# A decoder layer in split float32 on one core: another planned product length in the front, and other engines for splits and biases around the first layer norm

## The chip, the cores and the metric

One Trainium2 chip, one of its cores. The metric is the device time of one execution in microseconds (us), the median over several executions. Engines: PE (TensorE matmul), PEld (its weight loads), DVE (VectorE), ACT (ScalarE), POOL (GpSimd), SP (SyncE, which here only issues DMAs). [...]

## What is computed

One layer over 512 tokens of width 1024 in float32. With `h = x @ w_in` (1024 x 2560) split into q, k, v, u, z (512 wide each):

```python
attn = moba_attention(rope(q), rope(k), v)         # 8 heads of 64, blocks of 256 keys
u, z = gelu(u), gelu(z)
sg   = u * (tril(w_s) @ layer_norm(z) + b_s)       # per chunk of 128 positions, 8 groups
mix  = concat(rms_norm(attn), rms_norm(sg)) @ w_out
x    = layer_norm(2**0.25 * x + mix)               # first layer norm
x    = layer_norm(2**0.25 * x + (silu(x @ w_gate) * (x @ w_up)) @ w_down)
```

The hidden width of the last line is 2816.

## The kernel before, in words

**Split products.** Every large product runs on float32 values that are split into a high part (`hi`, stored as float32r) and a low part (`lo = value - hi`). One call of `mm3` (L250) issues three matmuls into one accumulating bank: hi*hi, hi*lo, lo*hi (L252, L253, L254). A product below is one such call, on a 128x512 output. A weight chunk of 128x1024 comes by one DMA of 512 KB (class `W`, L258 on) and is split by `split` (L235): the high part on ACT (L239) or, with `near`, on DVE (L237); the low part on DVE or, with `far`, on POOL (both L240). Which group of weights takes which engine stands in `WHI` (high part on DVE) and `WPOOL` (low part on POOL). Groups are named `q0` to `q3`, `z`, `u`, and `o0` to `o7` for the eight chunks of `w_out`.

**The planner.** The program first records every operation of every engine in a class `Order`, with a cost, a due rank (`base`, mostly from the table `RANK`; a smaller one goes first among the operations that are ready) and what it reads and writes. `plan` (L108) is a list scheduler: it plays the operations through on the recorded costs, engine by engine, and the order that it finds is the order in which each engine's instructions are issued. On the chip each engine runs its list strictly in that order and waits for semaphores. Buffers of one tag are handed out in program order (`admit`), so an operation can be kept waiting by an earlier part that holds the buffers of a tag. A product is recorded at cost `MM` = 0.681, a product of the gate and up weights (three matmuls of 256 columns, L850) at `MM256` = 0.36. Transfers are recorded at max(0.46, KB/352) plus 1.9.

**The front.** `SEQ` gives the parts: `q1 a1 q0 z q2 a0 u q3 s a2 a3`. `v_step` makes 32 products for v; `q0` to `q3` (`qk_proj`, L375 on) 16 products each and then a rope, whose halves are turned by four small DMAs (L366, L367 on DVE, L369 on SP, L371 on POOL); `z` and `u` (`tok_proj`) 32 products each; `a0` to `a3` the attention of two heads each (scores L432 and L433, transposes L471, values L488); `s` the spatial gating (L566) and its norm: a square on ACT (L584), a power on POOL (L282), a scaling on DVE (L586), transposes on PE (L591). Projections have rank 15 and so fill PE between the attention's steps at rank 4. The temporaries of ropes, squares and of the gating's norm share the tag `rt` with 5 buffers.

**Output projection and first layer norm.** `out_half(4)` multiplies the gating's half by `o4` to `o7`, `out_half(0)` the attention's half by `o0` to `o3`, four token tiles t of 128 each, 8 products to a tile and half. When tile t of the second half is done, `pa_done` (L752 on) calls `layer_norm` (L685 on): add (L756), statistics (L693), scale and shift on ACT (L706), gain on DVE (L708), bias (L717). `LN1` has a letter for each tile: with `P` the bias runs on POOL, with `A` on DVE. After the bias come transposes (L766), copies (L770), splits of the operands (L239, L240), and, for t = 2 and 3, sums of blocks (`combine`, L734 on).

**Gate and up products.** The weights of the first four pairs come early (`EARLY` = 4): eight blocks, numbered 0 to 7, filled by `whole` (L833). With letter `M` of `EARLY_LO` a block goes through `split_dram` (L244): ACT writes the high part (L246) and the negative of it as the low part (L247), and a DMA from POOL (L248) fetches the same 512 KB once more and adds it to the low part. With letter `D` the low part is one subtraction on DVE (L240), as elsewhere. Blocks 0 to 3 stand in buffers of their own, 4 to 7 in the ring `wh`, `wl`. After them 11 pairs run through 7 products of 8 steps each, and then the 22 chunks of the down projection (`down_mm`), which call `mm3` with the same `MM`.

Of the kernel before, what the change touches and what calls it, by code (L numbers as in the profile page):

```python
# [29 lines left out]

SAME, CROSS, DMA_LAT, MM, MM256 = 0.15, 0.19, 1.9, 0.681, 0.36
GROW, GROW_LAT = 0.9, 10
SEQ = ('q1', 'a1', 'q0', 'z', 'q2', 'a0', 'u', 'q3', 's', 'a2', 'a3')
RANK = {"w": 5.0, "rope": 10.0, "att": 4.0, "gelu": -8.0, "z": -2.0, "s": -13.5, "fill": 15.0, "sq": -6.0, "ln": -10.5, "ffn": 8.0, "evac": 3.0}


UNITS = (2, 0, 3, 1)
NORM = "AADA"  # L40
LN1, LN2, LNT = "APAA", "ADAD", 0.3
WHI = ('o0', 'o2', 'q1')
WPOOL = ('e0', 'e1', 'e3', 'o1', 'o2', 'o4', 'z')
ROPE, ZSUB, ZMUL, ZG, ZB = "P", "P", "P", "P", "P"


class Buf:
# [139 lines left out]
def build(tc, cp, wp, ap, ps, xt, xtok, w_vqk, w_zu, w_out, w_gu, w_dn, wsp, cst, rows, cols, out):  # L187
# [14 lines left out]
    def dma(kb, fn, r, w, **k):  # L202
        od.op("SP", max(0.46, kb / 352.0), fn, r, w, **k)

    def pe(n, fn, r, w, **k):
        od.op("PE", n, fn, r, w, **k)
# [10 lines left out]
    def prob(dtype=F32):  # L217
        return work([P, S], "pr", 4, dtype)
# [4 lines left out]
    def bank(tag, bufs):  # L223
        return od.buf(ps, [P, S], F32, tag, bufs)

    def pj():
        return bank("pj", 4)
# [7 lines left out]
    def split(n, src, hi, lo, rs, ws_hi, ws_lo, far=False, lock=True, near=False, **k):  # L235
        if near:
            dve(n, lambda: V.tensor_scalar(hi(), src(), 1.0, None, op0=ALU.mult), rs, ws_hi, per=0.52, lock=True, **k)  # L237
        else:
            act(n, lambda: A.activation(hi(), src(), AF.Copy), rs, ws_hi, **k)  # L239
        either("P" if far else "D", n, lambda E: E.tensor_tensor(out=lo(), in0=src(), in1=hi().bitcast(F32),  # L240
                                                                 op=ALU.subtract), [*rs, *ws_hi], ws_lo,
               lock=lock, **k)
# [7 lines left out]
    def mm3(cost, o, lh, ll, rh, rl, start, stop, r, w, **k):  # L250
        def fn():
            PE.matmul(o(), lhsT=lh(), rhs=rh(), start=start, stop=False)  # L252
            PE.matmul(o(), lhsT=lh(), rhs=rl(), start=False, stop=False)  # L253
            PE.matmul(o(), lhsT=ll(), rhs=rh(), start=False, stop=stop)  # L254

        pe(cost, fn, r, w, **k)

    class W:  # L258


        def __init__(self, src, tag=None, mid=None, group=None):
# [10 lines left out]
            every = slice(0, WCH)  # L272
            dma(512, lambda: nc.sync.dma_start(raw.t, src), [], [raw], base=RANK["w"])
            if mid is not None:
                mid(raw)
            split(WCH, lambda: raw.t, lambda: self.hi(every), lambda: self.lo(every), [raw], hk, lk, group in WPOOL,
                  near=group in WHI, base=RANK["w"])

# [14 lines left out]
    def row(i):  # L293
        b = work([P, D], "kl", 2)
        dma(512, lambda: nc.sync.dma_start(b.t, bass.AP(tensor=rows.tensor, offset=rows.offset + 3 * S + i * D,
                                                        ap=[[0, P], [1, D]])), [], [b], base=RANK["rope"])
        return b
# [16 lines left out]
    def v_step(c, kk, raw, wh, wl):  # L314
        k = 2 * c + kk
        cs = slice(kk * 512, kk * 512 + 512)
        xr = prob()
        dma(256, lambda: nc.sync.dma_start(raw.t[:, cs], w_vqk[c][:, cs]), [], [(raw, kk)], base=RANK["w"])
        split(512, lambda: raw.t[:, cs], lambda: wh.t[:, cs], lambda: wl.t[:, cs],
              [(raw, kk)], [(wh, kk)], [(wl, kk)], base=RANK["w"])  # L320
        pieces = ((0, 1), (1, NT)) if k == 0 else ((0, NT),)
        for t0, t1 in pieces:
            def piece(t0=t0, t1=t1, ts=slice(t0 * P, t1 * P)):
                sub = [(k, t) for t in range(t0, t1)]
                dma(64 * (t1 - t0), lambda: nc.sync.dma_start(xr.t[:, ts], xt[k][:, ts]), [], [(xr, t0)], base=RANK["w"])
                split((t1 - t0) * P, lambda: xr.t[:, ts], lambda: xh.t[:, k, ts], lambda: xl.t[:, k, ts], [(xr, t0)],
# [299 lines left out]
    def out_half(c0, spare, left, done, wide=None):  # L626
        ws = [W(w_out[c0 + k], spare if k == 3 else None, group=f"o{c0 + k}") for k in range(4)]
        for t in range(NT):
            ts = slice(t * P, t * P + P)
            b = [bank("sc", 2), bank("sc", 2)] if t == wide else [pj(), pj()]  # L630
            for k in range(4):
                for hf in range(2):
                    def one(k=k, hf=hf, t=t, ts=ts, b=b, hs=slice(hf * 512, hf * 512 + 512)):
                        lh, ll, keys = left(k, t, ts)
                        mm3(MM, lambda: b[hf].t, lh, ll, lambda: ws[k].hi(hs), lambda: ws[k].lo(hs), k == 0, k == 3,
                            [*keys, *ws[k].key], [b[hf]])

                    one()
            done(t, b)
# [277 lines left out]
            self.gated(c, self.h1, self.i1, 0, -1.0)  # L917

    pairs = [Pair(p) for p in range(NP)]
    EARLY, EARLY_LO = 4, "MMMMMMMM"  # L920
    EARLY_SLOTS = (("wr", "wr"), (0, 1), ("wr", "wr"), (0, 1))
    for p in range(EARLY):
        blks = [whole(Raw(p, 3 * i, EARLY_SLOTS[p][i]), 2 * p + i) for i in range(2)]
# [47 lines left out]
    yb = [[pj(), pj()], [pj(), pj()], [bank("sc", 2), bank("sc", 2)], [bank("tp", 1), bank("pv", 1)]]  # L971
# [3 lines left out]
    def down_w(f, tag=None):  # L975
        w = W(w_dn[f], tag)
        if f < FT - 4:
            hh, hl = prob(F32R), tmp(F32R)
            parts, keys = (lambda: hh.t, lambda: hl.t), ([hh], [hl])
        else:  # L980
            i = 2 * (FT - 1 - f)
            parts, keys = (lambda: last.t[:, i, :], lambda: last.t[:, i + 1, :]), ([(last, i)], [(last, i + 1)])
        h, hi = hT[f]
        hk, neg = [(h, (hi, t)) for t in range(2)], -1.0 if f % 2 else 1.0
        act(512, lambda: A.activation(parts[0](), h.t[:, hi, :], AF.Copy, scale=neg), hk, keys[0])
        dve(560, lambda: V.scalar_tensor_tensor(out=parts[1](), in0=h.t[:, hi, :], scalar=neg, in1=parts[0]().bitcast(F32),
                                                op0=ALU.mult, op1=ALU.subtract), [*hk, *keys[0]], keys[1], lock=True)
        return w, parts, keys[0] + keys[1]

    def down_mm(f, t, hf, w):  # L990
        w, (hh, hl), keys = w
        ts = slice(t * P, t * P + P)
        hs = slice(hf * 512, hf * 512 + 512)
        mm3(MM, lambda: yb[t][hf].t, lambda: hh()[:, ts], lambda: hl()[:, ts],
            lambda: w.hi(hs), lambda: w.lo(hs), f == 0, f == FT - 1, [*w.key, *keys], [yb[t][hf]])

    TAIL = 6
    for f in range(FT - TAIL):
        w = down_w(f)
        for t in (3, 0, 1, 2):  # L1000
            for hf in range(2):
                down_mm(f, t, hf, w)
# [3 lines left out]
    def finish(t):  # L1006
        for i in range(2):
            for f in wt:
                down_mm(f, t, i, wt[f])

        def add(i, key):
            dve(512, lambda: V.scalar_tensor_tensor(out=xk.t[:, t, HV[i]], in0=xk.t[:, t, HV[i]], scalar=ALPHA,
                                                    in1=yb[t][i].t, op0=ALU.mult, op1=ALU.add),
                [yb[t][i], key], [key])

        def done(i, key):
            dma(256, lambda: nc.sync.dma_start(out[t * P:t * P + P, HV[i]], xk.t[:, t, HV[i]]), key, [])

        od.base = RANK["ffn"] - 0.1 * (t + 1)
        layer_norm(t, add, done, LN2[t])  # L1020
        od.base = RANK["ffn"]
# [68 lines left out]
```

## Time and profile before

| | |
|---|---|
| median of 3 executions | 566.88 us (566.67 to 567.62) |
| profiled execution, its own time | 566.79 us |
| its span, first to last instruction | 565.0 us, so 1.79 us lie around it |
| mean granted PE clock | 0.986 |
| PE, DVE, ACT, POOL busy | 97%, 72%, 51%, 28% of the span |
| DMA | 72.85 MB, mean 129 GB/s |

The profiled execution is 0.09 us under the median. Busy PE is counted from the issue of matmuls whose ends are modelled; the idle time before a matmul is what its row shows in brackets, with the engine that released it. PE works in 40 slices at 90% or more except in two: the eleventh (about 141 to 155 us), at 6 tenths with a granted clock of 6 tenths, and the last.

### The profile page before, as it was taken

Reading aid. Unit: us, or ns where it says so; the run is one execution under the profiler, and the core shown is the slowest. Engines: PE = TensorE matmul, PEld = TensorE weight load, DVE = VectorE, ACT = ScalarE, POOL = GpSimd, SP = SyncE. Lnnn points to the kernel's source line nnn. Section 1 sums busy time; section 2 is a strip of 40 time slices with the busy share of each in tenths; the row PEclk is TensorE's granted clock in tenths of the full one; section 3 lists DMA queues with packets and bytes.
Section 4 is the critical chain, followed back from the end, with each engine's and each line's share of the span. In section 5 each row is a group of like instructions: output and inputs, shape, how many; then the busy total and the mean of one; then the engine's idle time right before and its main releaser. Section 6 shows DMA issues by size and latency. Waiting matters only on the chain.

```text
span 565.0 us, 8788 instructions
## 1 busy us (share of the span) xinstructions
PE 545.7 (97%) x3360; PEld 488.1 (86%) x3360; DVE 406.6 (72%) x701; ACT 290.0 (51%) x492; POOL 158.2 (28%) x120
## 2 busy tenths in 40 slices
PE   9999999999699999999999999999999999999994
PEld 6887888888488878999999999999999888888883
DVE  5645868889885879979998788878877623324485
ACT  6324787687774768745444544554455432323211
POOL 0016229823311531234452342333322200000011
PEclk9999999999699999999999999999999999999998
DMA  8746412144811898635432333233124333232311
GB/s 261 261 133 160 129 59 93 57 143 134 307 43 45 244 280 205 171 109 187 131 131 89 137 98 106 97 113 113 37 75 150 117 107 105 82 113 79 108 74 74
DMA packets 23241, 72.85 MB, mean 129 GB/s; under 512 B 3104, under 2 KB 3616, under 8 KB 23200
## 3 DMA queue, kind: packets, MB, share of 16 engines
q1 hardware_dynamic: 22048, 68.11, 37.2%
q0 software_dynamic: 1152, 4.19, 4.0%
q8 instruction: 26, 0.43, 0.3%
q14 instruction: 15, 0.12, 0.1%
HBM read 66.00 MB, written 2.10 MB: 121 GB/s over the span
## 4 chain that ended last, share of the span: by engine, by line
PE 84%; DMA 5%; ACT 5%; DVE 3%; issue 2%; SPq 1%; POOL 0%; DVEq 0%; POOLq 0%; ACTq 0%
PE pj L850 19%; PE sc L850 16%; PE pj L252 11%; PE pj L253 11%; PE pj L254 11%; DMA wr<-w_gu 2%; PE sc L252 2%; PE sc L253 2%; PE sc L254 2%; PE pv L488 2%; PE tp L471 1%; DMA wr<-w_out 1%; DMA zg<-w_gu 1%; DMA qk<-qk 1%; PE pv L252 1%
## 5 line engine op out<-in xcount | busy, mean ns | idle before, releaser
L240 DVE TENSOR_TENSOR wl<-wr,wh 128x1024 fp32r<-128x1024 f32 (+1 forms) x56 | 71.7, 1284 | 63.0 <-ACT wh L239 62.9
L239 ACT ACTIVATE wh<-wr 128x1024 fp32r<-128x1024 f32 (+1 forms) x59 | 58.9, 999 | 82.4 <-PE sc L254 54.0
L850 PE MATMUL pj<-qk,wh 128*128 128x256 f32 x352 | 64.4, 283 | 0.0
L850 PE MATMUL sc<-xh,wh 128*128 128x256 f32 x352 | 64.3, 283 | 0.0
L850 PEld LDWEIGHTS pj<-qk,wh 128*128 128x128 f32 x352 | 55.0, 192 | 0.0
L850 PEld LDWEIGHTS sc<-xh,wh 128*128 128x128 f32 x352 | 54.9, 192 | 0.0
L282 POOL TENSOR_TENSOR sm<-sm,only 128x1 f32<-128x1 f32 (+2 forms) x17 | 18.7, 1099 | 124.8 <-DVE sm L281 124.8
L850 PE MATMUL pj<-V,wh 128*128 128x256 f32 x288 | 52.6, 283 | 0.0
L850 PE MATMUL pj<-qk,wl 128*128 128x256 f32 x176 | 50.0, 284 | 0.1
L850 PE MATMUL sc<-xh,wl 128*128 128x256 f32 x176 | 49.9, 283 | 0.0
L252 PE MATMUL pj<-wh,xh 128*128 128x512 f32 x114 | 47.0, 412 | 0.0
L253 PE MATMUL pj<-wl,xh 128*128 128x512 f32 x114 | 45.0, 395 | 0.0
L850 PEld LDWEIGHTS pj<-V,wh 128*128 128x128 f32 x288 | 45.0, 192 | 0.0
L850 PE MATMUL pj<-V,wl 128*128 128x256 f32 x144 | 40.8, 283 | 0.0
L254 PE MATMUL pj<-wh,xl 128*128 128x512 f32 x96 | 37.9, 395 | 0.0
L240 POOL TENSOR_TENSOR wl<-wr,wh 128x1024 fp32r<-128x1024 f32 x7 | 17.7, 2523 | 69.5 <-ACT wh L239 66.6
L239 ACT ACTIVATE wh<-tp 128x512 fp32r<-128x512 f32 x33 | 19.6, 595 | 30.1 <-PE sc L850 20.4
L850 PEld LDWEIGHTS pj<-qk,wl 128*128 128x128 f32 x176 | 33.8, 192 | 0.3 <-DVE wl L240 0.3
L850 PEld LDWEIGHTS sc<-xh,wl 128*128 128x128 f32 x176 | 33.8, 192 | 0.0
L850 PE MATMUL sc<-ug,wh 128*128 128x256 f32 x176 | 32.2, 284 | 0.9 <-ACT wh L239 0.9
L850 PEld LDWEIGHTS sc<-ug,wh 128*128 128x128 f32 x176 | 27.5, 192 | 1.2 <-ACT wh L239 1.1
L253 PE MATMUL pj<-wl,pr 128*128 128x512 f32 x72 | 28.0, 390 | 0.0
(338 smaller groups left out, 1510.6 us busy)
## 6 DMA issues: line engine op xcount, KB each, us to landing
wr<-w_dn SPq DMA_DIRECT2D x22, 512.0 KB, 3.3
wr<-w_gu SPq DMA_DIRECT2D x20, 512.0 KB, 3.4
zg<-w_gu SPq DMA_DIRECT2D x18, 512.0 KB, 3.4
kl<-w_gu SPq DMA_DIRECT2D x14, 512.0 KB, 3.3
wr<-w_vqk SPq DMA_DIRECT2D x8, 512.0 KB, 3.6
wr<-w_zu SPq DMA_DIRECT2D x8, 512.0 KB, 3.5
wr<-w_out SPq DMA_DIRECT2D x8, 512.0 KB, 4.2
wr<-w_vqk SPq DMA_DIRECT2D x8, 256.0 KB, 4.5
```

The source lines that it names most:

```text
L239: act(n, lambda: A.activation(hi(), src(), AF.Copy), rs, ws_hi, **k)
L240: either("P" if far else "D", n, lambda E: E.tensor_tensor(out=lo(), in0=src(), in1=hi().bitcast(F32), op=ALU.subtract), [*rs, *ws_hi], ws_lo,
L252: PE.matmul(o(), lhsT=lh(), rhs=rh(), start=start, stop=False)
L253: PE.matmul(o(), lhsT=lh(), rhs=rl(), start=False, stop=False)
L254: PE.matmul(o(), lhsT=ll(), rhs=rh(), start=False, stop=stop)
L282: od.op("POOL", 0.3 + 0.165 * n, lambda: PL.tensor_tensor(out=o.t, in0=v.t, in1=mhalf.t[:, :n], op=ALU.pow), [v, mhalf], [o], lock=True)
L471: PE.transpose(tp.t[:, j * P:j * P + P], p.t[:, j * P:j * P + P], ident.t)
L488: PE.matmul(pv.t[:, j * P:], lhsT=vs.t[:, j, h, :], rhs=pt.t[:, j * S:j * S + w], start=j == 0 and i == 0, stop=j == NT - 1 and i == 1)
L850: PE.matmul(o, lhsT=lh(w), rhs=buf.t[:, s + rh, x], start=first and side == k == i == 0, stop=k == 3 and i == 2, skip_group_check=True)
```

## The change

The planner reckons the products of v, q, k, z and u at 0.643 instead of 0.681; those of the output and down projections keep 0.681 under a new name, `MMD`. Due ranks of the first layer norm, the gate and up products and their evacuations move. In the first layer norm the bias of tiles 0 and 2 goes to POOL and that of tile 1 to DVE; the ranks of the tiles lie closer (`LNT`). The high parts of `o1` and `o3` go from ACT to DVE. Early blocks 0 and 7 form their low part on DVE instead of by ACT and a second fetch. `EARLY` and `EARLY_LO` move to the top of the file.

```diff
-SAME, CROSS, DMA_LAT, MM, MM256 = 0.15, 0.19, 1.9, 0.681, 0.36
+SAME, CROSS, DMA_LAT, MM, MMD, MM256 = 0.15, 0.19, 1.9, 0.643, 0.681, 0.36
...
-RANK = {"w": 5.0, "rope": 10.0, "att": 4.0, "gelu": -8.0, "z": -2.0, "s": -13.5, "fill": 15.0, "sq": -6.0, "ln": -10.5, "ffn": 8.0, "evac": 3.0}
+RANK = {"w": 5.0, "rope": 10.0, "att": 4.0, "gelu": -8.0, "z": -2.0, "s": -13.5, "fill": 15.0, "sq": -6.0, "ln": -5.8, "ffn": 10.8, "evac": 4.6}
...
-LN1, LN2, LNT = "APAA", "ADAD", 0.3
-WHI = ('o0', 'o2', 'q1')
-WPOOL = ('e0', 'e1', 'e3', 'o1', 'o2', 'o4', 'z')
+LN1, LN2, LNT = "PAPA", "ADAD", 0.05
+WHI = ('o0', 'o1', 'o2', 'o3', 'q1')
+WPOOL = ('o1', 'o2', 'o4', 'z')
...
+EARLY, EARLY_LO = 4, "DMMMMMMD"
...
     def out_half(c0, spare, left, done, wide=None):
...
-                        mm3(MM, lambda: b[hf].t, lh, ll, lambda: ws[k].hi(hs), lambda: ws[k].lo(hs), k == 0, k == 3,
+                        mm3(MMD, lambda: b[hf].t, lh, ll, lambda: ws[k].hi(hs), lambda: ws[k].lo(hs), k == 0, k == 3,
...
-    EARLY, EARLY_LO = 4, "MMMMMMMM"
...
     def down_mm(f, t, hf, w):
...
-        mm3(MM, lambda: yb[t][hf].t, lambda: hh()[:, ts], lambda: hl()[:, ts],
+        mm3(MMD, lambda: yb[t][hf].t, lambda: hh()[:, ts], lambda: hl()[:, ts],
```

## Rows read from the trace of the kernel before

**Rows 1.** Page, busy us and share of the span, by engine.

```profile
PE 545.7 (97%) x3360; PEld 488.1 (86%) x3360; DVE 406.6 (72%) x701; ACT 290.0 (51%) x492; POOL 158.2 (28%) x120
```

**Rows 2.** Timeline of PE, 141 to 149 us: start, us, instruction, idle before it.

```profile
143.29 0.33 PE L471 MATMUL tp<-only,pr 128*128 128x128 f32 x1 [2.02 <-DVE sm L281]
...
146.35 1.12 PE L591 MATMUL pj<-only,ug 128*128 128x128 f32 x4 [2.74 <-DVE ug L586]
...
148.96 0.80 PE L252 MATMUL pj<-wh,znh 128*128 128x512 f32 x1 [0.64 <-ACT znh L239]
```

**Rows 3.** Windows: stretch, length, busy us of each engine, PEclk, DMA share, GB/s.

```profile
146.30:153.50 7.20, 6.50 (x20) 4.83 (x21) 5.94 (x14) 5.30 (x12) 3.72 (x3) 0.50 1.00 377
```

**Rows 4.** Timeline of DVE, POOL and ACT ahead of those waits.

```profile
139.40 0.68 DVE L367 TENSOR_TENSOR rt<-pj,cs 128x512 f32<-128x512 f32 x1
...
140.34 1.28 POOL L371 TENSOR_TENSOR rt<-rt,rt 128x512 f32<-128x512 f32 x1 [4.99 <-DMA rt<-rt]
...
142.32 0.62 ACT L584 ACTIVATE rt<-ug 128x512 f32<-128x512 f32 x1
```

**Rows 5.** Timeline of PE, 209 to 225 us, the matmuls that waited.

```profile
209.51 0.39 PE L850 MATMUL pj<-V,pth 128*128 128x256 f32 x1 [0.92 <-ACT V L239]
210.24 0.38 PE L850 MATMUL pj<-V,pth 128*128 128x256 f32 x1 [0.34 <-DVE V L240]
...
215.07 0.63 PE L766 MATMUL tp<-only,xl 128*128 128x128 f32 x4 [0.74 <-issue]
...
224.14 0.51 PE L850 MATMUL pj<-V,ptl 128*128 128x256 f32 x2 [0.61 <-ACT cs L872]
```

**Rows 6.** Timeline of ACT, 206 to 209 us.

```profile
206.48 1.06 ACT L246 ACTIVATE wh<-wr 128x1024 fp32r<-128x1024 f32 x1 [1.91 <-DMA wr<-w_gu]
...
208.87 0.59 ACT L239 ACTIVATE V<-tp 128x512 fp32r<-128x512 f32 x1
```

**Rows 7.** DMA of 186 to 236 us: queues (packets, MB, share of 16 engines), then an issue with its median landing in us.

```profile
q1 hardware_dynamic: 2039, 7.38, 43.8%
q0 software_dynamic: 1037, 3.79, 40.8%
...
znh<-w_gu POOLq DMA_DIRECT2D x2, 512.0 KB, 12.8
```

**Rows 8.** Waits of PE: us in total, times, longest.

```profile
PE sc L432 <- DMA qk<-qk: 1.1, 1, 1.1
```

**Rows 9.** Timeline of PE in the front: first matmuls of two successive products.

```profile
35.91 0.39 PE L252 MATMUL pj<-xh,wh 128*128 128x512 f32 x1
...
36.59 0.39 PE L252 MATMUL pj<-xh,wh 128*128 128x512 f32 x1
```

**Rows 10.** Groups of PE by form, 0 to 139.6 us: first matmuls of the products, count.

```profile
L252 PE MATMUL pj<-wh,xh 128*128 128x512 f32 x96 | 39.7, 414 | 0.0
...
L252 PE MATMUL pj<-xh,wh 128*128 128x512 f32 x64 | 25.7, 402 | 0.0
```

**Rows 11.** Window in the front, columns as in rows 3.

```profile
80.00:100.00 20.00, 20.00 (x98) 16.56 (x97) 17.65 (x43) 16.44 (x32) 16.44 (x12) 1.00 0.29 92
```

**Rows 12.** Single lines: durations (ns min/median/max); then DVE in the timeline, 186 to 193 us.

```profile
L237 DVE TENSOR_SCALAR wh<-wr x4: 686/694/695, 23.1 to 185.5; 128x1024 fp32r<-128x1024 f32 x4
...
L717 DVE TENSOR_TENSOR xl<-xl,kl x10: 643/684/687, 199.7 to 555.6; 128x512 f32<-128x512 f32 x10
L717 POOL TENSOR_TENSOR xl<-xl,kl x2: 1292/1295/1298, 203.1 to 206.0; 128x512 f32<-128x512 f32 x2
...
186.80 2.86 DVE L665 SCALAR_TENSOR_TENSOR xh<-atr,only,xh 128x512 fp32r<-128x512 f32 x1
...
189.77 1.22 DVE L240 TENSOR_TENSOR ug<-wr,ug 128x1024 fp32r<-128x1024 f32 x1
...
192.60 1.41 DVE L756 SCALAR_TENSOR_TENSOR xl<-pj,sm,xl 128x512 f32<-128x512 f32 x2 [1.62 <-PE pj L254]
```

**Rows 13.** Window in the sums of blocks, columns as in rows 3.

```profile
227.00:231.00 4.00, 4.00 (x36) 4.00 (x35) 4.00 (x8) 4.00 (x8) 0.00 (x0) 1.00 0.36 128
```

## The prediction, made before the changed kernel had run

> **What bounds the kernel now.** I read the page's busy times first: PE is busy 545.7 us, 97% of the span [rows 1]. So only the 19.3 us in which PE waits, and what a lower clock adds to its work, can be won. Then the timeline of PE shows where it waits, and the timelines of the other engines why. The change can reach three places.
>
> Place A, 141 to 149 us. PE waits 2.02, 2.74 and 0.64 us, 5.40 together [rows 2]. [...] Its cause: the projections, which fill PE, have run out, and the gating's norm, which releases the next filler (the output products), comes late. Its square on ACT starts at 142.32, just behind POOL's rope sum of 140.34 to 141.62 [rows 4]. Both use the tag `rt`, whose five buffers are handed out in program order, and the rope of q3 comes first. That sum had waited for its transfer, and the DVE product ahead of it ran only at 139.40 [rows 4], since ropes have the lowest rank there.
>
> Place B, 200 to 226 us, around the first layer norm. PE waits 0.92 + 0.34 = 1.26 us for the first operand, then 0.74 and 0.61 [rows 5]. ACT, which writes this operand at 208.87, had stood 1.91 us before weights that had not landed, at 206.48 [rows 6]. The 16 DMA engines are the cause behind it: from 186 to 236 us the queue of SP holds 43.8% and that of POOL 40.8% of them, though POOL's moves half the bytes; its transfers of 512 KB land after 12.8 us [rows 7].
>
> Place C: the first scores wait 1.1 us for a transfer [rows 8].
>
> **The change, part by part.**
>
> *Products reckoned at 0.643.* Two products start 0.68 us apart [rows 9], so the old 0.681 was right and the new one is 0.038 too short. Nothing runs faster; only the order changes. There are 96 + 64 = 160 such products up to 139.6 us [rows 10], so the plan is up to 160 x 0.038 = 6.1 us short of PE's real time at the end of the front. Where filler is at hand, the planner now puts more of it ahead of an operation that waits for a chain. That is what C lacks: 1.1 us is less than two products, and z's stand ready. No row says how many slip in, so I take the middle of 0 and -1.1, -0.5.
>
> For A the trace of before has no direct price. [...] Above, the plan's shortage leaves other engines' work behind: DVE is busy 17.65 of 20 us [rows 11], so 6.1 x 0.88 = 5.4 us of its work can be pushed past the end of the filler. What decides A (`rt` in program order, ropes at the lowest rank on DVE) is not edited, so I take 0, with the ends -8.65 and +5.4. SP issues the rope's four small transfers and the weights in one list, so their order moves with this one and is priced in the same ends. Output and down products keep their cost.
>
> *Blocks 0 and 7 on DVE.* Removed: two ACT passes (about 1.0 us each, as the 1.06 us of its twin [rows 6]), two POOL issues and two fetches. POOL's 40.8% of 50 us is 20.4 us of all 16 engines for eight fetches [rows 7], 2.55 us each; one less ahead of the late weights frees more than the 1.91 us for which ACT stood. So the 1.26 us go. Of 0.74 and 0.61, which come from the same backlog of ACT, I take half, 0.7. Added: two subtractions of 1.22 us on DVE, as the row at 189.77 [rows 12]. That of block 0 has until the first product at 209.5, and DVE stood idle 1.62 us before 192.60 [rows 12]: cost 0, or 1.22 if that cover is gone. That of block 7 falls into a stretch where DVE has no idle time, 4.00 of 4.00 us [rows 13]; behind it are queued the sums and splits for which PE comes next. It costs 0 to 1.2; I take 0.3, since it is wanted last of the eight.
>
> *Biases.* Four halves to POOL, two back to DVE. A half takes 0.684 us on DVE and 1.295 on POOL [rows 12]. For t = 1, whose transposes feed the first operand, each half comes 0.6 us sooner; for t = 0 the transposes come 1.2 us later, but PE has t = 3's products meanwhile. For t = 2, behind them, up to 1.2 us later: that is why only half of the later waits is booked. DVE is relieved of two halves, 1.4 us, POOL gets 2.6. SP is not involved.
>
> *High parts of o1 and o3 on DVE*, 0.69 us each [rows 12] in place of 1.06 on ACT. For o1 POOL's subtraction waits behind it, and starts no later. For o3 it stands ahead of the low part that ends at 190.99 and PE wants at about 191.65: slack 0.66, cost 0, or 0.7 with the slack gone.
>
> *Ranks, `LNT`, the groups e0, e1, e3.* The rank of the layer norm passes only that of squares and gelu, that of evacuations only the attention's, that of the gate and up products only ropes and row loads; no such pair waits on one engine together there. No weight has a group e. All 0.
>
> **Sum:** -0.5 (C) + 0 (A) - 1.26 - 0.7 + 0.3 (B) = -2.2 us. From the profiled execution, 566.79, this is 564.6; it lies 0.09 under the median, so against the runs 564.7. The single costs move this case between 563.4 (all of B and C) and 566.0.
>
> [...] While POOL subtracted beside it, the DVE operation of 186.80 took 2.86 us [rows 12], four times a half-width pass. [...]
>
> **The rivals.**
>
> *A closes.* If the planner puts the norm's square one wait earlier, the 2.02 us go and the clock need not fall: -2.02 - 3.25 = -5.3 more, 559.4. For it: the order of the whole front moves, and one wait decides. Against: program order of `rt`. Chance 0.20.
>
> *A widens (slower).* PE runs out of filler with up to 5.4 us of DVE work left, and all of that stands before the norm: 564.7 + 5.4 = 570.1. It decides from the point where the gap grows by over 3.3 us, for there 568.0 is passed. For it: DVE is nearly full up to 139 us. Against: the attention, behind A, has output products as filler. Chance 0.26.
>
> *DVE is held by POOL.* The two further halves on POOL hold DVE 2 x 1.295 = 2.6 us and spare it only 2 x 0.684 = 1.4; the 1.2 us left fall on the waits of B: 565.9. With the 0.7 of o3's lost slack it is 566.6. For it: the 2.86 us; against: the planner keeps POOL and such DVE passes apart in time. Chance 0.14.
>
> **How the numbers follow.** The forecast has 0.40. About 0.2% (1.1 us) is what a measurement of this kernel can tell from no change: 565.7 to 568.0. Faster: 0.37 of the forecast, all of A closing and 0.01 of the third, 0.58. Same: 0.03 of the forecast, 0.12 of the third, 0.02 of A widening a little, 0.17. Slower: 0.24 of A widening and 0.01 of the third with block 7's 1.2 us, 0.25. The range of 559.2 to 569.6 reaches into both A cases, and leaves out the half of A closing that wins more and the upper end of A widening, some 0.18. The forecast's own range is 563.4 to 566.0.
>
> **What would show it.** Right: eight fetches from POOL become six, ACT's wait of 1.91 us and PE's first wait at the gate and up products are gone, C's wait is about 0.6, and A stands as it was, with one stretch of clock 0.50 near 7 us. Wrong: A's waits differ by over 2 us either way, or a second stretch of lower clock appears; or DVE passes of over 1 us stand beside POOL's biases, and PE waits for `combine`.

## The result, and the profile after

The changed kernel takes 560.12 us, median of 4 executions (558.59 to 560.71); the kernel before, on the same chip, takes 567.07. The ratio is 0.9873, 95% interval 0.9851 to 0.9894: 1.3% faster. The profiled execution took 560.07 us, against 566.79 before.

The page of the kernel after, its span, its busy times by engine and the clock in 40 slices:

```profile
span 558.4 us, 8789 instructions
...
PE 542.9 (97%) x3360; PEld 484.8 (87%) x3360; DVE 411.1 (74%) x703; ACT 285.7 (51%) x488; POOL 155.6 (28%) x120
...
PEclk9999999999999999999999999999999999999998
...
q0 software_dynamic: 864, 3.15, 3.2%
```

The span is 6.6 us shorter. PE's busy time fell from 545.7 [rows 1] to 542.9, so PE waits 15.5 us instead of 19.3: 3.8 us are idle time, 2.8 us are work at a higher clock. The slice with a granted clock of 6 tenths is gone. Queue q0 (POOL's) moved 3.15 MB, six transfers of 512 KB: the two fetches of blocks 0 and 7 are gone.

Where in the span it was won is read from windows of the kernel before, and then of the kernel after (stretch, length, busy us of PE, PEld, DVE, ACT, POOL, then PEclk, the granted PE clock as a share of full speed, DMA share, GB/s):

```profile
136.00:160.00 24.00, 18.60 (x89) 15.03 (x88) 20.80 (x50) 18.80 (x42) 7.83 (x7) 0.79 0.75 238
...
200.00:226.00 26.00, 23.37 (x163) 20.98 (x161) 21.77 (x41) 20.33 (x32) 6.28 (x7) 1.00 0.97 239
226.00:262.00 36.00, 34.96 (x290) 34.58 (x289) 30.86 (x48) 21.00 (x36) 10.19 (x7) 1.00 0.49 150
```

```profile
136.00:160.00 24.00, 21.30 (x112) 16.41 (x111) 22.83 (x61) 19.18 (x43) 6.26 (x7) 1.00 0.63 190
...
200.00:226.00 26.00, 25.18 (x202) 24.20 (x201) 23.98 (x44) 23.46 (x38) 6.87 (x7) 1.00 0.69 182
226.00:262.00 36.00, 34.30 (x284) 33.84 (x283) 32.97 (x49) 18.46 (x32) 14.48 (x10) 1.00 0.45 147
```

Idle time of PE is the length less the first busy time. In 136 to 160 us (place A) it is 2.70, before 5.40, and the clock is 1.00, where before it was 0.79 over this stretch: 2.7 us of waits and the 2.8 us of clock, 5.5 in all (the 2.8 is the fall of PE's busy time over the whole span, put down here to A, the only stretch of lower clock that went). In 200 to 226 us (place B) it is 0.82, before 2.63. In 226 to 262 us it is 1.70, before 1.04, so B as a whole gave 1.15.

The waits behind these sums, in PE's timeline of the kernel after (start, us, instruction, idle before it and its releaser; line numbers here are two higher than before's):

```profile
27.95 0.50 PE L254 MATMUL pj<-xh,wh 128*128 128x512 f32 x1 [0.59 <-DVE V L242]
...
59.58 0.41 PE L434 MATMUL sc<-qk,kl 128*128 128x384 f32 x1 [0.23 <-DMA qk<-qk]
...
142.16 0.50 PE L254 MATMUL pj<-wh,znh 128*128 128x512 f32 x1 [0.99 <-ACT znh L241]
...
144.81 0.66 PE L593 MATMUL pj<-only,ug 128*128 128x128 f32 x4 [0.27 <-DVE ug L588]
...
147.03 0.50 PE L255 MATMUL pj<-wl,znh 128*128 128x512 f32 x1 [1.29 <-DVE sm L283]
...
202.39 0.66 PE L768 MATMUL pv<-only,xl 128*128 128x128 f32 x4 [0.82 <-DVE V L242]
...
227.05 0.50 PE L852 MATMUL pj<-V,wh 128*128 128x256 f32 x2 [0.69 <-ACT cs L874]
```

Where A had waits of 2.02 and 2.74 [rows 2], it has 0.99 and 1.29, and output products stand between them: the first waiting matmul, at 142.16, is already one of these. C's wait of 1.1 [rows 8] is 0.23, but a new one of 0.59 stands at 27.95. The waits of 0.92, 0.34, 0.74 and 0.61 [rows 5] are gone; 0.82 at 202.39 is the only one in B's first window, and 0.69 at 227.05 follows. Together: A -5.5, B -1.15, C with its successor -0.3, and +0.3 in the tail, -6.65 against 6.6 by the spans.

Why A closed is in the other engines' timelines, first DVE's of the kernel before, then those of the kernel after:

```profile
133.43 0.67 DVE L366 TENSOR_TENSOR rt<-pj,cs 128x512 f32<-128x512 f32 x1
...
134.02 0.48 DVE L566 SCALAR_TENSOR_TENSOR ug<-pj,only,ug 128x256 f32<-128x256 f32 x1
```

```profile
128.71 0.68 DVE L368 TENSOR_TENSOR rt<-pj,cs 128x512 f32<-128x512 f32 x1
...
129.83 0.67 DVE L369 TENSOR_TENSOR rt<-pj,cs 128x512 f32<-128x512 f32 x1
...
133.90 0.48 DVE L568 SCALAR_TENSOR_TENSOR ug<-pj,only,ug 128x256 f32<-128x256 f32 x1
...
135.80 1.30 POOL L373 TENSOR_TENSOR rt<-rt,rt 128x512 f32<-128x512 f32 x1 [1.31 <-DMA rt<-rt]
...
136.45 0.62 ACT L586 ACTIVATE rt<-ug 128x512 f32<-128x512 f32 x1
```

The part q3 has two ropes, one for q and one for k; what follows is the first. Its second DVE pass stands at 129.83, among the gating's passes (L568); before, it ran at 139.40 [rows 4], five us behind the last of them. POOL's sum, behind which the planner reckons an `rt` buffer free, follows at 135.80 instead of 140.34, and the norm's first square starts at 136.45 instead of 142.32. From the end of the last gating pass (133.90 + 0.48) to that square 2.1 us pass, and before 7.8 (134.02 + 0.48 to 142.32). On the chip the square does not wait for that sum: in the kernel after it starts 0.65 us before the row of the sum ends (135.80 + 1.30). What holds it is its place in ACT's list, and that place was fixed by the planner's reckoning of the buffer.

### The profile page after: what moved, and what is told of

Its sections match the earlier page's. It is cut to its first block, busy times and chain, and to the rows that moved or that the text cites. A ratio compares the mean times of both kernels' runs of the same rounds, so it can differ in the third digit from the quotient of the medians.

```text
span 558.4 us, 8789 instructions
## 1 busy us (share of the span) xinstructions
PE 542.9 (97%) x3360; PEld 484.8 (87%) x3360; DVE 411.1 (74%) x703; ACT 285.7 (51%) x488; POOL 155.6 (28%) x120
## 3 DMA queue, kind: packets, MB, share of 16 engines
q0 software_dynamic: 864, 3.15, 3.2%
## 4 chain that ended last, share of the span: by engine, by line
PE 90%; DMA 3%; DVE 3%; ACT 2%; issue 0%; DVEq 0%; ACTq 0%
PE pj L852 22%; PE sc L852 16%; PE pj L254 12%; PE pj L255 11%; PE pj L256 11%; DMA wr<-w_gu 2%; PE sc L254 2%; PE sc L256 2%; PE sc L255 2%; PE pv L490 2%; PE tp L473 2%; DMA qk<-qk 1%; PE sc L435 1%; PE pv L254 1%; PE pv L256 1%; PE tp L254 1%
## 5 line engine op out<-in xcount | busy, mean ns | idle before, releaser
L242 DVE TENSOR_TENSOR wl<-wr,wh 128x1024 fp32r<-128x1024 f32 (+1 forms) x56 | 69.9, 1249 | 61.7 <-ACT wh L241 61.4
L284 POOL TENSOR_TENSOR sm<-sm,only 128x1 f32<-128x1 f32 (+2 forms) x17 | 16.9, 992 | 141.6 <-DVE sm L283 141.5
L242 DVE TENSOR_TENSOR wl<-tp,wh 128x512 fp32r<-128x512 f32 x33 | 22.6, 684 | 8.2 <-ACT wh L241 7.9
```

What stands on the lines that cost most here:

```text
L284: od.op("POOL", 0.3 + 0.165 * n, lambda: PL.tensor_tensor(out=o.t, in0=v.t, in1=mhalf.t[:, :n], op=ALU.pow), [v, mhalf], [o], lock=True)
```

## The experiments

Twelve kernels were run, all of which compute the whole layer. The letters in the expectations stand for theories, in short: F, that the front's order alone makes the gain; G, that it needs the other edits; R, that the square's wait for `rt` is the cause of A; T, that the gain follows the planned length of a product as a trend; C, that a changed length only deals another order, good or bad; H, that late fetches ahead of POOL's small operations cost B its time.

### The front alone, and everything but the front

`e1_front_only`, from the kernel before:

```diff
-SAME, CROSS, DMA_LAT, MM, MM256 = 0.15, 0.19, 1.9, 0.681, 0.36
+SAME, CROSS, DMA_LAT, MM, MMD, MM256 = 0.15, 0.19, 1.9, 0.643, 0.681, 0.36
```

The output and down projections take `MMD`, as in the kernel after; nothing else is edited.

> The kernel before with one edit: products of v, q, k, z and u reckoned at 0.643. Theory F (the front's order alone closed place A): PE's waits between 140 and 160 us fall from 5.40 to about 2.7 us, no stretch at half clock there, the wait of the first scores falls to 0.2 or 0.3, and the time is 566.9 - 5.9 - 0.3 = about 560.7. Rival G (the lighter DMA and the other edits around the layer norm are needed for it as well): A keeps at least half of its cost, time 563.5 or more.

`e2_no_front`, from the kernel after:

```diff
-SAME, CROSS, DMA_LAT, MM, MMD, MM256 = 0.15, 0.19, 1.9, 0.643, 0.681, 0.36
+SAME, CROSS, DMA_LAT, MM, MMD, MM256 = 0.15, 0.19, 1.9, 0.681, 0.681, 0.36
```

> The changed kernel with those products back at 0.681, all else changed. Theory F: place A as in the kernel before (waits 5.4 us, some 7 us at half clock) and the gains of place B kept, about -1.2: 565.7. Rival G: A at least half closed without the new order, 563.5 or less.

Measured: e1 564.66 us, ratio to the kernel before 0.9943 (0.9913 to 0.9973); e2 572.37 us, 1.0078 (1.0049 to 1.0107), slower than before. Windows of e1, then one of its waits of PE (us in total, times, longest):

```profile
136.00:160.00 24.00, 21.49 (x113) 16.38 (x112) 22.50 (x60) 18.98 (x43) 7.73 (x7) 1.00 0.63 191
...
200.00:226.00 26.00, 24.42 (x194) 23.48 (x193) 22.65 (x43) 22.67 (x38) 5.45 (x7) 1.00 0.92 229
226.00:262.00 36.00, 32.90 (x268) 32.15 (x267) 31.84 (x45) 16.48 (x29) 14.21 (x9) 1.00 0.41 130
```

```profile
PE pj L850 <- DMA wl<-w_gu: 0.7, 1, 0.7
```

The front's order closes A by itself: 2.51 us idle and clock 1.00. But most of that is given back: idle time in 226 to 262 us is 3.10 (before 1.04), and 1.13 us in 262 to 300, where before has none. The wait shown is for a fetch into `wl`, the path that the changed kernel's block 7 no longer takes. So in e1 F is right about A and wrong about the time, and G the reverse.

In e2 place A is open again (5.83 us idle in 136 to 160, clock 0.86), and B is worse than before, 4.99 idle in 200 to 226. So F is right about A again and wrong that B's gain stays; G is wrong about both. Windows of e2, then ACT, POOL and PE in its timeline:

```profile
136.00:160.00 24.00, 18.17 (x92) 14.89 (x91) 22.71 (x52) 18.45 (x42) 6.96 (x7) 0.86 0.74 236
...
200.00:226.00 26.00, 21.01 (x125) 18.40 (x125) 19.06 (x34) 20.32 (x28) 12.69 (x12) 0.87 0.85 197
```

```profile
200.12 1.06 ACT L248 ACTIVATE pth<-wr 128x1024 fp32r<-128x1024 f32 x1 [7.15 <-DMA wr<-w_gu]
...
202.43 0.86 POOL L250 DMA_DIRECT2D znh<-w_gu  x1 [9.18 <-ACT znh L249]
202.99 0.88 POOL L284 TENSOR_TENSOR sm<-sm,only 128x1 f32<-128x1 f32 x1
...
207.52 1.12 PE L768 MATMUL tp<-only,xl 128*128 128x128 f32 x4 [3.91 <-POOL xl L719]
```

ACT waits 7.15 us for a weight block. The fetch that POOL issues for that block needs ACT's low part, so POOL stands 9.18 us, and the layer norm's power (L284), which reads none of this, is queued behind it on POOL and runs at 202.99. PE's first transposes wait 3.91 us at the end of that chain. POOL keeps to the order of its list here: the power, whose input DVE had written by 197.37, stays behind the fetch until 202.99.

The effects do not add. The front's new length is worth 2.3 us on the kernel before (566.9 for the kernel before, less 564.66) and 12.25 us with the other edits there (572.37 less 560.12). Those edits lose some 5 us without it and win 4.5 with it.

### Blocks 0 and 7 alone, and everything but them

`e3_early_only` sets `EARLY_LO` of the kernel before from "MMMMMMMM" to "DMMMMMMD"; `e4_no_early` sets that of the kernel after back.

> The kernel before with blocks 0 and 7 forming their low parts on DVE, nothing else. Theory D (fewer bytes bring the late weights sooner): ACT's wait of 1.91 us and PE's first wait of 1.26 us at the gate and up products go, time 565.5 to 566.0. Rival (DVE is the limit there): the two passes of 1.22 us on DVE take it back, 566.9 to 567.9.

> The changed kernel with all eight early blocks by the second fetch. Theory D: the first wait at the gate and up products comes back, 1 to 1.3 us, time 561.1 to 561.5. Rival (DVE is the limit): the time stays within 0.5 us of the changed kernel's 560.1 or falls.

Measured: e3 566.59 us, 0.9975 (0.9941 to 1.001): not told apart from no change. e4 563.62 us, 0.9945 (0.9919 to 0.9971), so taking this edit out of the kernel after costs 3.5 us. PE's timeline of e4 shows where (its profiled execution took 565.21 us, 1.6 above the median):

```profile
206.83 0.54 PE L852 MATMUL pj<-V,pth 128*128 128x256 f32 x1 [2.30 <-ACT V L241]
...
207.78 0.58 PE L852 MATMUL pj<-V,pth 128*128 128x256 f32 x1 [0.41 <-DVE V L242]
```

The wait at the first gate and up products, 0.92 + 0.34 before [rows 5], is back as 2.30 + 0.41, and the clock of 200 to 226 us falls to 0.87. That is theory D's wait, larger than D gave it; the rival is wrong here. In e3, idle time of 200 to 226 us falls from 2.63 to 1.99 and rises by 0.52 after it: the same repair, smaller. What is late behind it there was not traced.

### The cause at A, taken away directly

`e5_sq_bank` (from before) and `e6_after_sq_bank` (from after) write the norm's squares, of which only the sum is used, into the PSUM bank that the norm takes anyway, in place of an `rt` buffer:

```diff
-sq, ss, rs, tp = tmp(), small(1), small(1), pj()
+ss, rs, tp = small(1), small(1), pj()
...
-A.activation(sq.t, z(), AF.Square, accum_out=ss.t), [ug], [sq, ss], acc=True)
+A.activation(tp.t, z(), AF.Square, accum_out=ss.t), [ug], [tp, ss], acc=True)
```

> The kernel before; the squares of the gating's norm are written into the PSUM bank that the following transposes fill, and no longer take an rt buffer. Theory R (the square waited for an rt buffer that q3's rope holds): the first square starts by about 136 us instead of 142.3, PE's waits between 140 and 160 us fall from 5.40 to 2.7 us or less, and no stretch at half clock follows; the time is 561 to 565, as place B may lose up to 3.5 us again, as it did when the front's order alone was changed. Rival S (ACT and DVE are simply full there): the first square stays within 2 us of 142, and A costs 8 us or more.

> The changed kernel with the same squares in PSUM banks. Theory R: A's remaining waits of 2.70 us fall below 1.5 us; 557.5 to 560 where B does not move. Rival S: A keeps 2.7 us, 560 or more.

Measured: e5 582.92 us, 1.027 (1.0208 to 1.0331), 15.9 us slower; e6 566.92 us, 1.0001 (0.998 to 1.0023), 6.8 us over the kernel after. DVE, ACT and PE in the timeline of e5:

```profile
138.40 0.47 DVE L566 SCALAR_TENSOR_TENSOR ug<-pj,only,ug 128x256 f32<-128x256 f32 x1
...
139.51 0.59 ACT L584 ACTIVATE pj<-ug 128x512 f32<-128x512 f32 x1
...
155.37 0.68 DVE L366 TENSOR_TENSOR rt<-pj,cs 128x512 f32<-128x512 f32 x1
...
202.58 1.83 PE L674 MATMUL tp<-only,sqa 128*128 128x1 f32 x8 [4.11 <-DVE sqa L506]
```

Without `rt` the square starts 0.6 us behind the last gating pass (138.40 + 0.47 to 139.51), where it was 7.8: R's cause is shown. The gain isn't: idle time in 136 to 160 us falls to 3.27, at a clock of 0.93, but now q3's second rope comes last, at 155.37 (140.00 before), and with it the last attention. By then the output products no longer cover it (as I read the trace; it was not tried): PE waits 4.11 us for the last attention's sums, and 6.9 us for the bias ahead of the first transposes, as PE's waits of e5 have it:

```profile
PE tp L766 <- POOL xl L717: 6.9, 1, 6.9
```

In e6 q3's first rope stays early (passes at 127.24 and 128.36) and the first square starts at 133.17, yet 3.18 us are idle in 136 to 160, at a clock of 1.00, against 2.70 in the kernel after. So `rt` is not what is left of A there, and by the numbers written for e6 it is S that came true. A is as good as in the kernel after, and the 6.8 us are lost elsewhere: 3.75 us are idle in 200 to 226, at a clock of 0.93. Why B loses there was not traced. A closed place A is thus not enough for the time: the same edit deals out what comes behind it anew.

### Fetches reckoned late, and other lengths of a product

`e7_no_front_lat6` (from e2) and `e8_after_lat6` (from after) record the arrival of the weights of blocks 0 and 3 of the first four pairs at 6.0 us instead of 1.9 after the transfer, so the planner places what waits for them later:

```diff
+if p < EARLY and j in (0, 3) and slot != 'x': od.ops[-1].lat = EARLY_LAT
```

> The kernel with all but the front's order changed (572.4), and the planner reckoning the arrival of the eight early weight blocks 6.0 instead of 1.9 behind their transfer. Theory H (in that kernel the layer norm's power stood on POOL behind the issue of a second fetch that waited for late weights): the fetch is then issued behind the powers and the biases, PE's wait of 3.9 us at the first transposes and the lower clock behind it are gone, time 565.5 to 567.5. Rival (the bias on POOL is itself too slow): a wait of 2 us or more stays at the first transposes, 569.5 or more.

> The changed kernel with the same 6.0. Theory H: its wait of 0.8 us at the transposes goes and B gains up to 1.5 us: 558.6 to 560. Rival (the order fitted B by its own numbers, and any other loses): 561.5 or more.

Measured: e7 568.95 us, 1.0041 (1.0014 to 1.0068), 3.4 under e2, with intervals that overlap; e8 561.52 us, 0.9903 (0.9871 to 0.9935), 1.4 over the kernel after, and also overlapping. POOL in the timeline of e7:

```profile
199.15 0.56 POOL L284 TENSOR_TENSOR sm<-sm,only 128x1 f32<-128x1 f32 x1 [4.53 <-DVE sm L283]
```

The power, at 202.99 in e2, now runs at 199.15, ahead of the fetch, which is issued at 206.26. In PE's waits of e7 the 3.91 of e2 are 1.8, idle time in 200 to 226 us falls from 4.99 to 2.46:

```profile
PE tp L768 <- POOL xl L719: 1.8, 1, 1.8
```

The mechanism of H is there. The time lies between the two forecasts, about half of H's gain and not resolved from none (the profiled execution, 571.85 us, is 2.9 above the median); the biases on POOL are late next. In e8 the wait of 0.82 us at the transposes goes, as H says, but PE waits 1.51 us for ACT at 218.51, idle time in 200 to 226 us is 2.16 instead of 0.82, and the time is the rival's, though not resolved from the kernel after.

`e9_after_066` and `e10_after_062` set `MM` of the kernel after to 0.66 and 0.62.

> The changed kernel with the front's products reckoned at 0.66. Theory T (any shorter duration that puts q3's rope on DVE among the spatial gating closes A): as at 0.643, PE's waits between 140 and 160 us stay at 2 to 3.5 us with no stretch at half clock, time 559 to 562. Rival C (each duration gives an order of its own, and no trend): A's waits above 4.5 us or a half-clock stretch, or a new wait elsewhere, time 564 or more.

> The changed kernel with 0.62, where q3's rope stands on DVE behind the gating's first scalings. Theory T in its plain form (the shorter the better covered): 559 to 562. Rival C: the rope of q3, and with it the last attention, comes late; a wait of 2 us or more before the output products of the attention's half or the first layer norm, time 564 or more.

Measured: e9 574.92 us, 1.0125 (1.0089 to 1.0161), and e10 587.48 us, 1.0358 (1.0318 to 1.0399). Ordered by `MM`, with the other edits in place: 0.62 gives 587.5, 0.643 560.1, 0.66 574.9, 0.681 572.4. There is no trend. Windows of e9, and then POOL in its timeline:

```profile
136.00:160.00 24.00, 20.16 (x107) 15.64 (x106) 22.87 (x49) 16.81 (x37) 4.08 (x6) 1.00 0.68 219
...
200.00:226.00 26.00, 18.75 (x116) 16.50 (x115) 21.61 (x43) 21.41 (x32) 10.36 (x11) 0.87 0.72 164
```

```profile
199.01 0.92 POOL L250 DMA_DIRECT2D znh<-w_gu  x1 [5.46 <-ACT znh L249]
199.65 0.88 POOL L284 TENSOR_TENSOR sm<-sm,only 128x1 f32<-128x1 f32 x1
```

At 0.66 place A keeps its clock, as T says, with 3.84 us idle; but in B PE is idle 7.25 us, 4.17 of it before the matmul at 211.27. The power stands once more behind a fetch, here one that waited 5.46. Its input was written by 197.62, so the fetch holds it up about 2 us; how the rest of the 7.25 comes about was not traced. At 0.62 A itself is open (6.84 idle, clock 0.76 in 136 to 160) and B too. There q3's first rope is early as well (126.91 and 127.52), but the gating's passes end only at 143.64 and the second rope starts at 158.54: an early first rope does not close A by itself. T falls, C holds.

### The biases, and the high parts of o1 and o3

`e11_no_ln` sets `LN1` and `LNT` of the kernel after back to "APAA" and 0.3. `e12_no_whi` sets `WHI` back to ('o0', 'o2', 'q1').

> The changed kernel with the biases as before (tile 1 on POOL, tiles 0 and 2 on DVE) and the old spacing of the ranks. Theory (POOL's biases relieve DVE where it is full): DVE gains 1.4 us of work, PE waits 1 us more in place B, 561 to 562.5. Rival (POOL's biases hold DVE up, by the 2.6 to 3.9 us that two of them were seen to take): 558 to 559.5.

> The changed kernel with the high parts of o1 and o3 on ACT as before. By the step as predicted (costs 0 both ways): 559.6 to 560.8. Rival (ACT, which then stands before late weights, is the engine that gains): a wait of 1 us or more before the output products of the attention's half or in B, 561.2 or more.

Measured: e11 561.22 us, 0.991 (0.9877 to 0.9942): 1.1 us over the kernel after, the theory's direction, but not resolved. e12 567.31 us, 1.0001 (0.9978 to 1.0023): with the two passes of 0.69 us back on ACT nothing of the gain is left, and the rival holds. A is still closed in e12 (2.93 us idle in 136 to 160, clock 1.00); idle time in 200 to 226 us is 3.79, and the clock there 0.87. PE and ACT in the timeline of e12, and a window of it:

```profile
198.46 0.60 PE L768 MATMUL tp<-only,xl 128*128 128x128 f32 x4
...
201.53 1.06 ACT L248 ACTIVATE wh<-wr 128x1024 fp32r<-128x1024 f32 x1 [3.47 <-DMA wr<-w_gu]
...
203.44 0.58 ACT L772 ACTIVATE pr<-tp 128x512 f32<-128x512 f32 x1
...
205.28 0.66 PE L768 MATMUL tp<-only,xl 128*128 128x128 f32 x4 [2.30 <-DVE V L242]
...
207.20 1.12 PE L768 MATMUL pv<-only,xl 128*128 128x128 f32 x4 [1.26 <-DVE V L242]
```

```profile
208.00:212.00 4.00, 3.78 (x16) 3.17 (x15) 3.97 (x9) 3.20 (x5) 1.02 (x2) 0.50 1.04 258
```

And ACT in the timeline of the kernel after, at the same place:

```profile
197.75 0.57 ACT L772 ACTIVATE pr<-tp 128x512 f32<-128x512 f32 x1
...
199.58 1.06 ACT L248 ACTIVATE wh<-wr 128x1024 fp32r<-128x1024 f32 x1 [0.76 <-DMA wr<-w_gu]
```

In the kernel after, ACT copies the first transposes and then takes the weights' split, which waits 0.76 us for its block. In e12 the split comes first in the list, waits 3.47 us, and the transposes of 198.46 are copied at 203.44; PE waits 2.30 and 1.26 us for what follows, and runs at half its clock behind it. That is one inversion of two ACT operations. How two moved passes of `o1` and `o3` lead the planner to it, and whether it carries all of the 7.2 us, was not tried.

## Why the prediction was right or wrong

**Place A: wrong, and it carries the difference.** The step that failed is "What decides A (`rt` in program order, ropes at the lowest rank on DVE) is not edited, so I take 0". The cause was right (e5 starts the square 0.6 us after the gating), and program order and ranks are as they were. But a rank only decides among operations that are ready, and in the changed order the passes of q3's first rope find their place on DVE 4.7 and 9.6 us earlier (128.71 and 129.83; before 133.43 and, [rows 4], 139.40). That the shorter length alone brings this about is shown by e1 (128.62 and 129.74); which choice of the planner did it, by a product that ends sooner in its reckoning, was only argued. The rival "A closes" put the square one wait earlier and priced it at -5.3; 5.5 were measured, and the time it gave, 559.4, is 0.7 from the median. That it comes so near is partly luck, for its split was another: it took away one wait whole and the clock fall; in the trace two waits were halved and the clock fall went. The clock was priced at 3.25 us; no run shows that term, nor the -8.65 that adds it to the 5.40 us of waits [rows 2]: PE's busy time fell by 2.8 us. In the stretch at 0.50 [rows 3] a product took 1.28 us in the kernel before, from its first matmul at 152.12 to the next instruction at 153.40, against 0.68 in the front [rows 9]:

```profile
152.12 0.63 PE L252 MATMUL pj<-wh,znh 128*128 128x512 f32 x1
...
153.40 0.79 PE L591 MATMUL pj<-only,ug 128*128 128x128 f32 x4
```

**The bound above for A** (up to 5.4 us of other engines' work left behind) did not come true at 0.643. That the direction was open is shown by 0.62, where A's idle time is 6.84 us, above the 5.40 of before.

**Place C:** -0.5 as written, -0.3 measured. The wait fell to 0.23, further than the 0.6 expected, and 0.59 of the gain went to the new wait at 27.95.

**Place B:** -1.7 as written, -1.15 measured. The waits named are gone, and what was late next took 0.7 back in 226 to 262 us. Eight fetches became six. ACT's wait before late weights did not go: it is 3.01 us at 190.98 and 0.76 at 199.58. The long one costs little: the layer norm's scale and shift behind it start at 192.90, and the DVE operation that releases them ends at 192.39 (192.25 + 0.14). The short one still costs: the copy and the split of the next transposes stand behind it, and PE's 0.82 at 202.39 is the end of that chain:

```profile
201.64 0.69 DVE L242 TENSOR_TENSOR V<-pv,V 128x512 fp32r<-128x512 f32 x1 [0.90 <-ACT V L241]
```

So the weights still come late for ACT, and the reason given (one fetch fewer brings them sooner) is not seen; what an equal wait costs depends on what is queued behind it. Two readings behind that reason were off: the 12.8 us to landing are those of two of POOL's eight fetches, the others took 7.1 and 9.3, and the queue moved 3.79 MB in that stretch [rows 7], which is 7.2 transfers and not eight, 2.8 us each. Alone, the edit does nothing that can be measured (e3); with the others it is worth 3.5 us (e4).

**High parts of o1 and o3: "cost 0" failed.** PE has no idle time in 160 to 200 us of the kernel after, so there is no sign of the 0.7 that o3's slack might have cost. But as an edit to a planned kernel it is worth 7.2 us (e12), more than the whole gain. The error is in the kind of step: each edit was costed by its own durations in the old order, while it deals out a new one.

**Ranks: 0 was right.** With the ranks alone edited, or the ranks of the changed kernel alone set back, the planner issues the same lists on all five engines. **Biases:** relief was forecast for DVE, and 1.1 us, not resolved, is what taking it away costs (e11).

**The rivals that did not happen.** DVE is held by POOL in places (below), but without PE waiting for `combine`. "A widens" is what 0.62 does.

**The signs written down.** Six fetches from POOL and the end of the first wait at the gate and up products came as forecast. ACT's wait, 0.6 for C and an A that stands as it was did not, and the sign of being wrong (A's waits differ by over 2 us) is there: 5.40 became 2.70.

**The range** of 559.2 to 569.6 held the result because it reached into "A closes"; the forecast's own range of 563.4 to 566.0 did not, so the time alone does not speak for the mechanism. The 0.40 went to an A that stands still while the whole front is issued anew, for which no row spoke; the 0.20 for the rival looks small beside it.

## What to carry to other kernels

In a kernel whose order is planned, a planned cost is a handle on the order and not a price: 0.643 won 6.9 us, and 0.62, 0.66 and 0.681 with the same edits lost between 5 and 21 against the kernel before. So sum up an edit by its instructions only where the order is known to stay (compare the issue lists first), and otherwise give the largest stall in the trace a wide chance of both going and growing. Then look, in the list of each engine, for an operation that waits for a late transfer with short critical operations queued behind it: that pattern set B in e2 (the power ran 5.6 us after its input was written) and in e12 (the copy 4.4 us after its transposes, 198.46 + 0.60 to 203.44) and had a part in e9, whatever had been edited.

## What the runs showed of the hardware

**The clock.** Waits of 0.99, 0.27 and 1.29 us with products between them left the granted clock at 1.00 in the kernel after. Waits of 2.02 and 2.74 [rows 2] were followed by 7.2 us at 0.50 [rows 3], and 2.30 and 1.26 in e12 by 0.50 in 208 to 212 us. About as much of the gain at A was clock (2.8 us) as was waiting (2.7).

**DVE beside POOL.** Timeline of the kernel after, POOL's biases and two runs of one DVE operation, the second beside them:

```profile
192.25 0.14 DVE L699 SCALAR_TENSOR_TENSOR sm<-sm,sm 128x1 f32<-128x1 f32 x1
...
194.82 2.71 POOL L719 TENSOR_TENSOR xl<-xl,kl 128x512 f32<-128x512 f32 x2
...
195.04 1.25 DVE L699 SCALAR_TENSOR_TENSOR sm<-sm,sm 128x1 f32<-128x1 f32 x1
```

The same operation takes 0.14 us alone and 1.25 beside POOL. Not every operation is held: the add of L758 took 1.40 us for two at 196.21 beside the biases, and its twin 1.41 with none beside it [rows 12]. In the timeline of e8 the two biases themselves take longer, 3.91 instead of 2 x 1.295 [rows 12]:

```profile
194.30 3.91 POOL L719 TENSOR_TENSOR xl<-xl,kl 128x512 f32<-128x512 f32 x2 [2.17 <-DVE xl L710]
```

Why some operations are held and others not was not shown. Moving two halves back to DVE in e11 was not faster (561.22 us against 560.12, not resolved), so no run shows that these longer passes decided the time.
